# One input projection reordered: all four channel tiles per chunk of tokens, k-tile by k-tile

## The chip, the core and the metric

The kernel runs on one core of a Trainium2 chip. The metric is the device time of one execution in microseconds (us), the median of several runs. The engines of the core work side by side, each with its own queue of instructions: TensorE (PE, with its weight loads shown apart as PEld), VectorE (DVE), ScalarE (ACT), GpSimd (POOL) and SyncE (SP), which here issues most of the transfers. [...]

## The reference

One step of a decoder layer for 1024 prompt tokens and 8 x 8 sample tokens, 1088 rows of 1024 channels. The change touches only the first of the products below, the 512 channels `a`.

```python
u = rms_norm(x, ln1)
a, q, k, v, g_a, g_b = split(u @ w_in)          # w_in: 1024 x 4864; a is 512 wide
branch_a = pooling of a over trailing windows 2/4/8/16, per-group linear map, scale
branch_b = dilated window attention of q, k, v in three groups of heads
h = x + (sigmoid(g_a) * (branch_a @ w_pa) + sigmoid(g_b) * (branch_b @ w_pb)) @ w_o
y = h + relu(rms_norm(h, ln2) @ w_up)**2 @ w_down
```

## The kernel before

Activations are held with channels on the partitions: eight k-tiles of 128 channels by 1088 tokens. For precision, each fp32 operand of a large product is split in two parts, hi (ScalarE, a copy to fp32r) and lo (VectorE, the remainder), and each product is three matmuls: hi x hi, hi x lo, lo x hi. `PASSES` lists them as (weight part, activation part).

The tokens go in three chunks (`CHUNKS`): 384, 384 and 320. The projection to `a` has four output tiles of 128 channels. Two weight panels hold them, 256 channels each: panel a0 gives tiles 0 and 1, panel a1 tiles 2 and 3. A panel is split into one of three `places` in SBUF; its raw fp32 pieces of 128 x 512 (two k-tiles) pass through three `raw` buffers in turn (`fetch`, line 127), so a fourth fetch waits until the first piece has been split (lines 116 and 117). The places are reused in turn by the q, k and v panels of the next stage, whose first matmul on PE is at line 632.

The order of work in the first stage:

- Twelve warm-up matmuls (line 360). Meanwhile x of chunk 0 is loaded, a pair of k-tiles at a time (`load_x`, 384 KB; the first pair as two loads), and panel a0 between.
- Panel a0 over chunks 0, 1, 2: `pool_input(0, wt, c)`, 48 matmuls per chunk (line 334), pair of k-tiles by pair, all passes of a pair before the next. `split_x` (lines 312 and 313) makes the hi and lo parts of a chunk's x. `pool_evac` copies the two tiles out of PSUM (lines 346 and 351).
- Panel a1 over chunks 0, 1, 2 in the same way.
- Between these, `square_x` squares a chunk's x in place on ACT (line 304) and adds the eight k-tiles up on POOL (line 306); `x_sums` then has PE sum over partitions (`rt`, line 369), and VectorE and POOL turn the sums into norms (lines 373 to 375).

PSUM: the accumulators of this stage are four banks in turn. A chunk of one panel uses two of them, so the next chunk finds the other two free.

The order on PE is the order of the program. On the other engines, and on SP, a scheduler at build time sets the order from a simulated timeline; each engine then keeps that order strictly. `behind_pe(instruction, mm)` holds an instruction until a given matmul is done (without `mm`, the last one issued so far). x of chunks 1 and 2 is loaded as early as its place in the SP queue allows.

Of the kernel before, what the change touches and what calls it, by code (L numbers as in the profile page):

```python
# [7 lines left out]
F32 = mybir.dt.float32  # L8
F32R = mybir.dt.float32r
AF = mybir.ActivationFunctionType  # L10
ALU = mybir.AluOpType
# [4 lines left out]
P = 128  # L16
D = 1024
SEQ = 1024
NB, NT = 8, 8
TOK = SEQ + NB * NT  # L20
KD = D // P
CH = 384
# [5 lines left out]
HD = 64  # L28
# [9 lines left out]
def decoder_step(ctx, tc, i, o):  # L38
    nc = tc.nc
    v_, s_, g_, t_ = nc.vector, nc.scalar, nc.gpsimd, nc.tensor  # L40
    dma = nc.sync.dma_start
# [49 lines left out]
    def part4(c):  # L91

        return slice(CHUNKS[c][0] // 4, (CHUNKS[c][0] + CHUNKS[c][1]) // 4)
# [12 lines left out]
    def from4(t, sub="p r l -> p l r"):  # L106
        return t.rearrange("p (r l) -> p r l", r=4).rearrange(sub)
# [4 lines left out]
    place = [0]  # L112
    throttle = []

    def split(dst_hi, dst_lo, src):
        ins = s_.activation(dst_hi, src, AF.Copy)  # L116
        v_.tensor_tensor(dst_lo, src, dst_hi.bitcast(F32), op=ALU.subtract)  # L117
        return ins

    def fetch(src, name, a, tied=False):  # L120
        raw = rr(wp, [P, 512], F32, name=f"raw_{name}_{a}", tag="raw", bufs=3)
        if callable(src):
            ins = dma(raw.rearrange("p (k n) -> p k n", k=4), src(a))
            if tied:
                behind_pe(ins)
        else:
            dma(raw, src[:, a:a + 512])
        return raw
# [121 lines left out]
    def acc_tile(name, tag="acc", bufs=4):  # L250
        return rr(acc_p, [P, 512], F32, name, tag, bufs)
# [17 lines left out]
    def win(name):  # L269
        return rr(xp, [P, LS], F32, name, "win", 2)  # L270
# [17 lines left out]
    def load_x(c, j):  # L288
        c0, n = CHUNKS[c]
        x = rr(xq, [P, 2, CH], F32, name=f"xs{c}_{j}", tag="xs", bufs=12)  # L290
        if c + j == 0:

            dma(x[:, 0, :n], i["xT"][:, 0, c0:c0 + n])
            dma(cols, i["cols"])
        else:
            dma(x[:, :, :n], i["xT"][:, 2 * j:2 * j + 2, c0:c0 + n])
        xs[c, "t", j] = x[:, :, :n]
        for k in range(2):
            xs[c, 2 * j + k] = x[:, k, :n]

    def square_x(c):
        t = [xs[c, "t", j] for j in range(4)]
        for j in (3, 0, 1, 2):
            behind_pe(s_.activation(t[j], t[j], AF.Square))
        for j in range(3):
            g_.tensor_tensor(t[3], t[3], t[j], op=ALU.add)

    def split_x(c, k):
        c0, n = CHUNKS[c]
        hi, lo = (act4[s][k][:, :, part4(c)] for s in range(2))  # L310
        x = xs[c, k].rearrange("p (l r) -> p r l", r=4)
        s_.activation(hi, x, AF.Copy, scale=ln1[:, k:k + 1])  # L312
        v_.scalar_tensor_tensor(lo, x, ln1[:, k:k + 1], hi.bitcast(F32), op0=ALU.mult, op1=ALU.subtract)

    def first(j):
        if j:
            load_x(0, j)
        else:
            dma(xs[0, 1], i["xT"][:, 1, :CH])
        split_x(0, 2 * j)  # L320
        split_x(0, 2 * j + 1)

    L = 15 + SEQ
    LS = L + NB * 23
    exts = {}

    def pool_input(ja, wt, c, middle=None):
        c0, n = CHUNKS[c]
        pts = [acc_tile(f"a{2 * ja + m}_{c}") for m in range(2)]
        for k in range(0, KD, 2):  # L330
            for p, (a, b) in enumerate(PASSES):
                for m in range(2):
                    for kk in (k, k + 1):
                        last_mm[0] = t_.matmul(  # L334
                            pts[m][:, :n], wt[:, a, kk, m * P:(m + 1) * P], act4[b][kk][:, :, part4(c)],
                            start=(p == 0 and kk == 0), stop=(p == 2 and kk == KD - 1))
            if middle and k == 4:
                middle()
        return pts

    def pool_evac(ja, c, pts):
        c0, n = CHUNKS[c]
        for m in range(2):
            ext = exts[2 * ja + m]
            npr = min(n, SEQ - c0)
            s_.copy(ext[:, 15 + c0:15 + c0 + npr].rearrange("p (l r) -> p l r", r=4),
                    from4(pts[m][:, :n])[:, :npr // 4])
            if npr < n:
                new = from4(pts[m][:, :n])[:, npr // 4:].rearrange("p (t q) r -> p q r t", q=2)
                for q in range(2):  # L350
                    s_.copy(ext[:, L:].rearrange("p (b t) -> p b t", b=NB)[:, 4 * q:4 * q + 4, 15:], new[:, q])
# [7 lines left out]
    for _ in range(12):  # L359
        t_.matmul(wu, ones, ones, start=True, stop=True)  # L360
    load_x(0, 0)
    wt = by_k(panel(i["w_in"][0], "a0", first))
    def x_sums(c):
        n = CHUNKS[c][1]
        rt = [rr(ps, [P, 1], F32, name=f"rt{c}_{b}", tag="rt", bufs=3) for b in range(3)]
        for b in range(3):
            w = min(P, n - b * P)
            for k in range(2):
                t_.matmul(rt[b][:w], xs[c, 6 + k][:, b * P:b * P + w], ones[:, :1], start=(k == 0), stop=(k == 1))
        for b in range(3):  # L370
            w = min(P, n - b * P)
            col = slice(3 * c + b, 3 * c + b + 1)
            v_.tensor_scalar(xms[:w, col], rt[b][:w], 1.0 / D, EPS, op0=ALU.mult, op1=ALU.add)
            g_.tensor_tensor(rtok[0][:w, col], xms[:w, col], mhalf[:w, :1], op=ALU.pow)
            v_.tensor_scalar(xeps[0][:w, col], xms[:w, col], EPS, None, op0=ALU.mult)
# [33 lines left out]
            v_.tensor_scalar(xeps[g][:, :8], xg, EPS, None, op0=ALU.mult)  # L409

    v_.memset(rtok[0], 0.0)
    for c in range(3):
        if c < 2:
            for j in range(4):
                load_x(c + 1, j)
        if c == 0:
            open_ext(0)
            open_ext(1)
        pool_evac(0, c, pool_input(0, wt, c))
        if c < 2:  # L420
            for k in range(KD):
                split_x(c + 1, k)
        if c:
            square_x(c - 1)
    square_x(2)
    w1 = by_k(panel(i["w_in"][1], "a1"))
    dma(cst, i["consts"])
    v_.tensor_scalar(wqs, wqc, HD ** -0.5, None, op0=ALU.mult)
    dma(states, i["stateT"].rearrange("g p b t -> p g (b t)"))
    kn = win("kn")[:, :P]  # L430
    for g in range(3):
        dma(kn[2 * g:2 * g + 2], i["qk_norm"][g, 1].rearrange("(j d) -> j d", j=2))
    open_ext(2)
    open_ext(3)
    for c in range(3):
        pool_evac(1, c, pool_input(1, w1, c, (lambda: x_sums(2)) if c == 2 else None))
        if c == 0:
            x_sums(0)
            sample_rows()
        if c == 1:  # L440
            x_sums(1)

            wk = rr(ps, [P, 512], F32, name="wk", tag="wu", bufs=1)[:, :6]
            t_.transpose(wk, kn[:6], ident[:6, :6])
            v_.tensor_tensor(wqk, wqs, wk, op=ALU.mult)
    moving = by_residue()
    next(moving)
    px.close()
# [722 lines left out]
    for g in (2, 1, 0):  # L1171
# [42 lines left out]
        for blks in ((8, 0), (1,), (2,), (3,), (4,), (5,)) + (((6, 7),) if g else ((6,), (7,))):  # L1214
# [12 lines left out]
            for js in (((0, 1), (2,)) if blks[0] in (1, 2, 3, 4, 5) else ((0,), (1,), (2,))):  # L1227
                for b in (blks[::-1] if g < 2 and js == (2,) and 8 in blks else blks):
# [1039 lines left out]
```

## Time and profile before

| | |
|---|---|
| median of 3 runs | 1400.61 us (1399.87 to 1401.57) |
| profiled execution | 1399.09 us, of which the span of the profile is 1397.3 us |
| TensorE busy | 1390.2 us |
| VectorE busy | 954.0 us |
| ScalarE busy | 756.1 us |
| GpSimd busy | 258.3 us |
| first projection matmul | 6.09 us from the span's start |
| first matmul of the next stage (line 632) | 61.03 us |

The profile is of one execution. "Busy" adds up the times in which an engine had an instruction under way; TensorE's matmuls are pipelined and overlap in the list, so the spacing of their starts says what one costs. In a timeline row stand the start, the duration of the (merged) instructions, the engine, the source line, the operation, the tensors written and read, the shapes and the count; in square brackets stands how long the engine was idle before it and who released it. L334 is line 334 of the kernel. A queue that ends in q (SPq) is the issue of transfers, not their landing.

### The profile page before, as it was taken

Reading aid. Unit: us, or ns where it says so; the run is one execution under the profiler, and the core shown is the slowest. Engines: PE = TensorE matmul, PEld = TensorE weight load, DVE = VectorE, ACT = ScalarE, POOL = GpSimd, SP = SyncE. Lnnn points to the kernel's source line nnn. Section 1 sums busy time; section 2 is a strip of 40 time slices with the busy share of each in tenths; the row PEclk is TensorE's granted clock in tenths of the full one; section 3 lists DMA queues with packets and bytes.
Section 4 is the critical chain, followed back from the end, with each engine's and each line's share of the span. In section 5 each row is a group of like instructions: output and inputs, shape, how many; then the busy total and the mean of one; then the engine's idle time right before and its main releaser. Section 6 shows DMA issues by size and latency. Waiting matters only on the chain.

```text
span 1397.3 us, 29307 instructions
## 1 busy us (share of the span) xinstructions
PE 1390.2 (99%) x11101; PEld 1341.6 (96%) x11101; DVE 954.0 (68%) x1707; ACT 756.1 (54%) x1787; POOL 258.3 (18%) x362
## 2 busy tenths in 40 slices
PE   9999999999999999999999999999999999999998
PEld 8988987888999999999999999999999999999998
DVE  7788744776876776975559677765665686664565
ACT  8557875787764224554337454554554544444443
POOL 0854356676500000000010000000000000000100
PEclk9999999999999999999999999999999999999999
DMA  6456886755587777956369668765768987777674
GB/s 216 133 166 211 245 246 195 231 139 137 149 248 232 244 220 257 318 194 211 130 199 296 222 217 290 245 204 204 250 202 287 319 274 257 238 239 230 211 256 170
DMA packets 180445, 311.96 MB, mean 223 GB/s; under 512 B 26696, under 2 KB 82318, under 8 KB 178255
## 3 DMA queue, kind: packets, MB, share of 16 engines
q1 hardware_dynamic: 174670, 258.04, 57.8%
q0 software_dynamic: 5632, 52.04, 11.6%
q8 instruction: 87, 1.43, 0.4%
q14 instruction: 56, 0.45, 0.1%
HBM read 239.94 MB, written 122.12 MB: 259 GB/s over the span
## 4 chain that ended last, share of the span: by engine, by line
PE 98%; ACT 0%; DMA 0%; POOL 0%; SPq 0%; issue 0%; DVE 0%; DVEq 0%
PE pz L1330 24%; PE pd L2113 24%; PE pg L1330 12%; PE ph L205 7%; PE pqk L205 6%; PE pab L1330 5%; PE pv L205 5%; PE a L334 3%; PE pk L205 2%; PE pq L205 2%; PE sg0b L702 1%; PE pog0b L735 1%; PE pl L513 1%; PE tpg0b L721 1%; PE sg1b L702 0%; PE tpg1b L721 0%
## 5 line engine op out<-in xcount | busy, mean ns | idle before, releaser
L2113 PE MATMUL pd<-places 128*128 128x272 f32 x2688 | 331.7, 287 | 0.0
L2113 PEld LDWEIGHTS pd<-places 128*128 128x128 f32 x2688 | 331.6, 188 | 0.0
L116 ACT ACTIVATE places<-raw_d 128x544 fp32r<-128x544 f32 (+1 forms) x176 | 110.6, 646 | 159.1 <-DMA raw_d<-z_d 54.8
L2166 POOL DMA_DIRECT2D out_kv_sample_dram<-in_cache_kv_dram x96 | 46.9, 489 | 791.1 <-ACT places L116 582.2
L117 DVE TENSOR_TENSOR places<-raw_d,places 128x544 fp32r<-128x544 f32 (+1 forms) x176 | 122.4, 710 | 90.8 <-ACT places L116 89.0
L1330 PE MATMUL pz<-act,places 128*128 128x280 f32 (+1 forms) x1080 | 139.4, 287 | 0.0
L1330 PEld LDWEIGHTS pz<-act,places 128*128 128x128 f32 x1080 | 135.9, 188 | 0.0
L205 PE MATMUL ph<-act,places 128*128 128x280 f32 (+1 forms) x768 | 96.6, 287 | 0.0
L205 PEld LDWEIGHTS ph<-act,places 128*128 128x128 f32 x768 | 96.0, 188 | 0.1
L1330 PE MATMUL pg<-act,places 128*128 128x264 f32 (+1 forms) x576 | 75.6, 288 | 0.0
L1330 PEld LDWEIGHTS pg<-act,places 128*128 128x128 f32 x576 | 72.6, 188 | 0.6 <-issue 0.3
L1330 PE MATMUL pz<-places,apart 128*128 128x264 f32 (+1 forms) x528 | 67.9, 287 | 0.0
L1330 PEld LDWEIGHTS pz<-places,apart 128*128 128x128 f32 x528 | 66.6, 188 | 0.0
L205 PE MATMUL pqk<-places,act 128*128 128x512 f32 x240 | 60.6, 402 | 0.0
L1330 PE MATMUL pz<-act,apart 128*128 128x264 f32 (+1 forms) x456 | 59.1, 287 | 0.0
L1330 PEld LDWEIGHTS pz<-act,apart 128*128 128x128 f32 x456 | 57.5, 188 | 0.1
L661 POOL TENSOR_TENSOR mr<-ms,mhalf 128x4 f32<-128x4 f32 (+2 forms) x39 | 54.7, 1403 | 2.9 <-POOL ms L660 0.2
L205 PEld LDWEIGHTS pqk<-places,act 128*128 128x128 f32 x240 | 44.8, 192 | 9.6
L886 POOL TENSOR_TENSOR pck<-pck,qs 128x256 f32<-128x256 f32 x64 | 48.6, 791 | 21.1 <-DVE sta L711 12.4
L334 PE MATMUL a<-act,places 128*128 128x384 f32 (+1 forms) x288 | 50.5, 333 | 1.7 <-ACT act L312 1.1
L334 PEld LDWEIGHTS a<-act,places 128*128 128x128 f32 x288 | 47.6, 188 | 3.8 <-ACT act L312 1.9
L1330 PE MATMUL pab<-ab,places 128*128 128x264 f32 (+1 forms) x384 | 50.4, 286 | 0.0
(438 smaller groups left out, 2805.8 us busy)
## 6 DMA issues: line engine op xcount, KB each, us to landing
out_kv_sample_dram<-in_cache_kv_dram POOLq DMA_DIRECT2D x72, 480.0 KB, 5.0
raw_d<-z_d SPq DMA_DIRECT2D x112, 272.0 KB, 4.2
z_d<-t SPq DMA_DIRECT2D x80, 272.0 KB, 3.7
raw_d<-in_w_down_dram SPq DMA_DIRECT2D x80, 256.0 KB, 4.1
raw_u<-in_w_up_dram SPq DMA_DIRECT2D x64, 256.0 KB, 4.3
raw_qkv<-in_w_in_dram SPq DMA_DIRECT2D x36, 256.0 KB, 4.3
own_d<-in_cache_kv_dram POOLq DMA_DIRECT2D x32, 256.0 KB, 3.8
pck<-own_d SPq DMA_DIRECT2D x16, 512.0 KB, 4.8
```

The lines of the kernel that those rows point to most:

```text
L116: ins = s_.activation(dst_hi, src, AF.Copy)
L117: v_.tensor_tensor(dst_lo, src, dst_hi.bitcast(F32), op=ALU.subtract)
L205: last_mm[0] = t_.matmul(out, lhs(a, k), rhs(b, k), start=(j == 0), stop=(j == len(terms) - 1))
L334: last_mm[0] = t_.matmul(pts[m][:, :n], wt[:, a, kk, m * P:(m + 1) * P], act4[b][kk][:, :, part4(c)], start=(p == 0 and kk == 0), stop=(p ...
L513: t_.matmul(pl[:, :npr], lin[:, g, :], dp_[:, c0:c0 + npr], start=True, stop=True)
L661: last_norm[0] = g_.tensor_tensor(r[:n, :H], ms[:n, :H], mhalf[:n, :H], op=ALU.pow)
L702: t_.matmul(sc[e][:, hp, j * P:(j + 1) * P], qT[rows, hp, :], kT[rows, 2 + hp, :], start=True, stop=True)
L721: t_.transpose(tp[:, hp * nk + j, :], sms[e][:, hp, j * P:(j + 1) * P], ident)
L886: ins = g_.tensor_tensor(out, *others, op=ALU.mult)
L1330: last_mm[0] = t_.matmul(out[c], lhs(*term), rhs(*term, c), start=(first and n == 0), stop=(n == len(terms) - 1), skip_group_check=not first)
L2113: last_mm[0] = t_.matmul(chain[t][c], A[:, a, t * P:(t + 1) * P], Z[:, b, c], start=(fresh and f == 0 and n == 0), stop=(f == NG - 1 and n ...
L2166: ins = g_.dma_start(d, a)
```

## The change

The projection now runs once per chunk with all four tiles, instead of once per panel and chunk. In chunks 0 and 1 the first six k-tiles go pair by pair over both panels and all four accumulators (24 matmuls on a pair), and the last two k-tiles then tile by tile, so that each tile is finished and copied out by itself. Chunk 2 goes tile by tile over all k-tiles. In chunk 0, panel a0, the odd k-tiles take the lo part of the weights ahead of the lo part of x (`BY_WEIGHT`).

Both panels' pieces are fetched in turn with x of chunk 0, whose k-tiles are now loaded singly (192 KB). x of chunk 1 is loaded behind the end of panel a1's matmuls on k-tiles 2 and 3 of chunk 0 (`in_chunk[0, 3]`), x of chunk 2 behind a1's on k-tiles 4 and 5 (`in_chunk[0, 5]`); the hi splits of chunk 1 wait for a0's matmuls on k-tiles 4 and 5 (`in_chunk[0, 4]`). The constants, states and norms are loaded behind the end of chunk 0. The squares and row sums move with the new order: `x_sums` runs after tile 0, after tile 1, and two thirds into tile 3 of chunk 2.

```diff
-            dma(x[:, :, :n], i["xT"][:, 2 * j:2 * j + 2, c0:c0 + n])
+            behind_pe(dma(x[:, :, :n], i["xT"][:, 2 * j:2 * j + 2, c0:c0 + n]), mm)
...
-        s_.activation(hi, x, AF.Copy, scale=ln1[:, k:k + 1])
+        ins = s_.activation(hi, x, AF.Copy, scale=ln1[:, k:k + 1])
+        if c == 1:
+            behind_pe(ins, in_chunk[0, 4])
...
+    def first_panels():
+        wts = []
+        for _ in range(2):
+            wts.append(places[:, place[0] % 3])
+            place[0] += 1
+        for j in range(4):
+            if j:
+                t = rr(xq, [P, 2, CH], F32, name=f"xs0_{j}", tag="xs", bufs=12)
+                xs[0, "t", j] = t
+                for k in range(2):
+                    xs[0, 2 * j + k] = t[:, k]
+                dma(t[:, 0], i["xT"][:, 2 * j, :CH])
+            raw = [fetch(i["w_in"][0], "a0", 512 * j)]
+            dma(xs[0, 2 * j + 1], i["xT"][:, 2 * j + 1, :CH])
+            raw.append(fetch(i["w_in"][1], "a1", 512 * j))
+            for ja in range(2):
+                split_x(0, 2 * j + ja)
+                ins = split(*(wts[ja][:, s, 512 * j:512 * j + 512] for s in range(2)), raw[ja])
+        throttle.append(ins)
+        return [by_k(w) for w in wts]
...
+    BY_WEIGHT = ((0, 0), (1, 0), (0, 1))
...
+        begun = 6 if c < 2 else 0
+        for k in range(0, begun, 2):
+            for ja in range(2):
+                for kk in (k, k + 1):
+                    for p, (a, b) in enumerate(BY_WEIGHT if c == 0 and ja == 0 and kk else PASSES):
+                        for m in range(2):
+                            mm(2 * ja + m, a, b, kk, kk == 0 and p == 0, False)
+                in_chunk[c, k + ja] = last_mm[0]
+        for t in range(4):
+            for p, (a, b) in enumerate(PASSES):
+                for k in range(begun, KD):
+                    mm(t, a, b, k, p + k == 0, p == 2 and k == KD - 1)
+                if p == 1 and (t, 1) in then:
+                    then[t, 1]()
+            pool_evac(t, c, pts[t])
+            if t in then:
+                then[t]()
...
+    THEN = ({}, {0: lambda: split_chunk(2), 1: lambda: square_x(1), 3: lambda: square_x(2)},
+            {0: lambda: (x_sums(0), sample_rows()), 1: lambda: (x_sums(1), key_norms()), (3, 1): lambda: x_sums(2)})
     for c in range(3):
+        pool_input(c, THEN[c])
         if c == 0:
+            for cc in range(1, 3):
+                for j in range(4):
+                    load_x(cc, j, in_chunk[0, 3] if cc == 1 else in_chunk[0, 5])
+            split_chunk(1)
+            square_x(0)
+            behind_pe(dma(cst, i["consts"]))
```

More of the change, by code (lines that the diff above doesn't have):

```diff
@@ L286, in decoder_step, with load_x @@
     xs = {}
-    def load_x(c, j):
+    def load_x(c, j, mm=None):
         c0, n = CHUNKS[c]
@@ L325, in decoder_step, with pool_input @@
     exts = {}
-    def pool_input(ja, wt, c, middle=None):
+    BY_WEIGHT = ((0, 0), (1, 0), (0, 1))
+    in_chunk = {}
+    def pool_input(c, then={}):
         c0, n = CHUNKS[c]
-        pts = [acc_tile(f"a{2 * ja + m}_{c}") for m in range(2)]
-        for k in range(0, KD, 2):
-            for p, (a, b) in enumerate(PASSES):
[L332 to L339, printed above, removed]
@@ L341, in pool_evac @@
-    def pool_evac(ja, c, pts):
-        c0, n = CHUNKS[c]
[L343 to L351, printed above, removed]
+        pts = {}
@@ new lines, in mm @@
+        def mm(t, a, b, k, start, stop):
+            ja, m = divmod(t, 2)
+            if t not in pts:
+                pts[t] = acc_tile(f"a{t}_{c}")
+            last_mm[0] = t_.matmul(pts[t][:, :n], wt[ja][:, a, k, m * P:(m + 1) * P], act4[b][k][:, :, part4(c)],
+                                   start=start, stop=stop)
+        begun = 6 if c < 2 else 0
[6 more added lines that the diff above has]
+                in_chunk[c, k + ja] = last_mm[0]
@@ new lines, in pool_input, with pool_evac @@
+        for t in range(4):
+            for p, (a, b) in enumerate(PASSES):
+                for k in range(begun, KD):
[5 more added lines that the diff above has]
+                then[t]()
+    def pool_evac(t, c, pt):
+        c0, n = CHUNKS[c]
+        ext = exts[t]
+        npr = min(n, SEQ - c0)
+        s_.copy(ext[:, 15 + c0:15 + c0 + npr].rearrange("p (l r) -> p l r", r=4), from4(pt[:, :n])[:, :npr // 4])
+        if npr < n:
+            new = from4(pt[:, :n])[:, npr // 4:].rearrange("p (t q) r -> p q r t", q=2)
+            for q in range(2):
+                s_.copy(ext[:, L:].rearrange("p (b t) -> p b t", b=NB)[:, 4 * q:4 * q + 4, 15:], new[:, q])
@@ L361, in decoder_step @@
     load_x(0, 0)
-    wt = by_k(panel(i["w_in"][0], "a0", first))
+    wt = first_panels()
     def x_sums(c):
```

52 lines of the change are left out of this document (14 added, 38 removed).

## The prediction

> **What bounds the kernel now.** I read the page's totals first, then its chain of work that ended last, then the timeline of the first 61 us engine by engine, because the diff touches nothing behind that point.
>
> ```profile
> span 1397.3 us, 29307 instructions
> PE 1390.2 (99%) x11101; PEld 1341.6 (96%) x11101; DVE 954.0 (68%) x1707; ACT 756.1 (54%) x1787; POOL 258.3 (18%) x362
> PE 98%; ACT 0%; DMA 0%; POOL 0%; SPq 0%; issue 0%; DVE 0%; DVEq 0%
> ```
>
> TensorE sets the time nearly everywhere. The change alters no number of matmuls, so it can only win time in which TensorE stands still between its first projection matmul and the first matmul of the next stage (line 632), or lose by making it stand still more. So I price the real matmuls and compare them with the clock. In the timeline of PE (start, duration, engine, line):
>
> ```profile
> 6.09 0.44 PE L334 MATMUL a<-act,places 128*128 128x384 f32 x1 [0.59 <-ACT places L116]
> 6.98 2.46 PE L334 MATMUL a<-act,places 128*128 128x384 f32 x11 [0.45 <-ACT act L312]
> 9.68 0.44 PE L334 MATMUL a<-act,places 128*128 128x384 f32 x1 [0.24 <-ACT act L312]
> 10.55 30.90 PE L334 MATMUL a<-act,places 128*128 128x384 f32 x179 [0.42 <-ACT act L312]
> 41.29 1.39 PE L369 MATMUL rt<-ones,xs 128*128 128x1 f32 x12
> 42.54 8.73 PE L334 MATMUL a<-act,places 128*128 128x384 f32 x48
> 51.11 1.39 PE L369 MATMUL rt<-ones,xs 128*128 128x1 f32 x12
> 52.58 5.55 PE L334 MATMUL a<-act,places 128*128 128x320 f32 x36
> 57.97 1.27 PE L369 MATMUL rt<-ones,xs 128*128 128x1 f32 x12
> 59.17 2.02 PE L334 MATMUL a<-act,places 128*128 128x320 f32 x12
> 61.03 0.28 PE L632 MATMUL pq<-places,smp_t 128*128 128x256 f32 x1
> ```
>
> Durations overlap, so I go by starts. 48 matmuls of 384 columns take 51.11 - 42.54 = 8.57 us, 0.1785 each; 36 of 320 columns take 57.97 - 52.58 = 5.39, 0.150 each. The projection has 192 of the first and 96 of the second kind: 34.3 + 14.4 = 48.7 us. The row sums (rt) with the small transpose cost 1.25 + 1.47 + 1.20 = 3.9. Work: 52.6 us. Clock: 61.03 - 6.09 = 54.9. So TensorE loses 2.3 us here, and 2.1 of them by 10.55, where 13 matmuls (2.3 us of work) have taken 4.46. **That 2.3 us is the most this change can win.** It lies where each k pair of chunk 0 waits for its split, since before only 12 matmuls (2.1 us) stand on a pair.
>
> **Part 1: chunk 0 with all four tiles.** A k pair now carries 24 matmuls, 4.3 us, but also needs a second panel's piece. These are the splits (ACT hi, DVE lo) and the arrivals:
>
> ```profile
> 5.41 0.63 ACT L116 ACTIVATE places<-raw_a 128x512 fp32r<-128x512 f32 x1 [1.02 <-DMA raw_a<-in_w_in_dram]
> 5.95 0.98 ACT L312 ACTIVATE act<-xs,cols 128x384 fp32r<-128x384 f32 x1
> 7.24 0.63 ACT L116 ACTIVATE places<-raw_a 128x512 fp32r<-128x512 f32 x1 [0.31 <-DMA raw_a<-in_w_in_dram]
> 8.65 1.85 ACT L312 ACTIVATE act<-xs,cols 128x384 fp32r<-128x384 f32 x2 [0.77 <-DMA xs<-in_xT_dram]
> 6.07 0.69 DVE L117 TENSOR_TENSOR places<-raw_a,places 128x512 fp32r<-128x512 f32 x1 [0.74 <-ACT places L116]
> 6.96 0.92 DVE L313 SCALAR_TENSOR_TENSOR act<-xs,cols,act 128x384 fp32r<-128x384 f32 x1 [0.20 <-ACT act L312]
> ```
>
> The first matmul still needs x0 and the first weight piece, whose loads keep their places: 6.09. The order by weight lets the first four matmuls go on x0 alone; only the twelfth needs x1's lo part, ready at 6.96 + 0.92 = 7.88, so twelve are done at about 8.24, with no loss. The second panel's first piece takes the fetch that landed at 7.24. From there ACT needs 0.98 + 0.63 = 1.6 us per k, 12.9 for eight, and DVE 0.92 + 0.69 = 1.6; PE needs 12 x 0.1785 = 2.14 per k. PE is the slower, and chunk 0 would end at 8.24 + 84 x 0.1785 = 23.2. That is the whole 2.3 us, if the transfers keep up.
>
> They are 8 x 192 KB of x and 8 x 256 KB of weights, 3.67 MB. Only three raw buffers turn over; the fourth fetch waits, and x loads queue on SP behind it:
>
> ```profile
> 6.79 0.34 SPq L127 DMA_DIRECT2D raw_a<-in_w_in_dram  x1
> raw_a<-in_w_in_dram SPq DMA_DIRECT2D x8, 256.0 KB, 5.3
> DMA to landing us min/median/max: 2.8/4.3/6.8
> 0.00:5.00 5.00, 3.94 (x21) 3.94 (x22) 1.09 (x9) 2.47 (x3) 0.20 (x4) 1.00 0.48 122
> 5.00:10.00 5.00, 3.72 (x18) 2.53 (x16) 2.98 (x5) 3.50 (x5) 0.00 (x0) 1.00 1.01 342
> ```
>
> (The last two rows are windows; their last column is GB/s.) A buffer's turn is landing + 0.63 + 0.69 us. At 2.8 the fourth fetch, issued at 6.8, is split by 10.9, and PE wants it at 12.5; at the 5.3 that pieces took under the full load of before, it lands at 12.1, and PE waits 0.2 to 1 us on this turn and the next. At 6.8 it would lose about 3. The queue is emptier in the new order, so I take the lower end, a loss of 0.2.
>
> At 342 GB/s the 3.67 MB need 10.7 us, well inside the 17 of chunk 0. [...]
>
> **Part 2: chunk 1 behind chunk 0.** The loads wait on SP for chunk 0's 48th matmul, 8.24 + 36 x 0.1785 = 14.7. Behind them on SP stand chunk 2's loads, the constants, states, norms and then the next stage's weights; none of those is wanted before 40 us. The splits wait on ACT for the 60th matmul, 16.8. With a landing of 2.8, x arrives from 17.5; at 0.98 + 0.92 a pair's splits are done by about 20.4, and PE wants them at 23.2: a cover of 2.8 us, lost only if landing takes 5.6 or more.
>
> The four accumulators are another matter. Before, a chunk used two banks of four and the next had the other two; now all four are full when chunk 1 begins, and its first two matmuls need tiles 0 and 1 copied out. Those copies share ACT with the splits:
>
> ```profile
> 14.97 5.39 ACT L312 ACTIVATE act<-xs,cols 128x384 fp32r<-128x384 f32 x6
> 20.26 0.83 ACT L346 COPY ext<-a 128x384 f32<-128x384 f32 x2
> 20.99 7.96 ACT L312 ACTIVATE act<-xs,cols 128x384 fp32r<-128x384 f32 x10
> ```
>
> Here the copies ran at 20.26 behind six splits of the next chunk, though 48 matmuls were done by about 17.2 (10.55 + 35 x 0.1785 = 16.8 and the last one's 0.34). That cost nothing with two spare banks. In the new order tiles 0 and 1 finish at 20.0 and 21.1. With none of the eight splits ahead the cost is nothing; with six ahead, from 17.5 at 0.90 each, the copies end at 23.7, 0.5 us late; with all eight at 25.5, 2.3 late. I take the middle one, nearest to what ACT's order was: 0.5. [...]
>
> **Part 3: the end.** The row sums of x sit after tile 0, after tile 1 and two thirds into tile 3 of chunk 2. Each needs four squares on ACT and three adds on POOL:
>
> ```profile
> 30.63 3.05 ACT L304 ACTIVATE xs<-xs 128x768 f32<-128x768 f32 x4
> 32.30 16.72 POOL L306 TENSOR_TENSOR xs<-xs,xs 128x768 f32<-128x768 f32 x8 [31.85 <-ACT xs L304]
> 56.45 2.03 POOL L374 TENSOR_TENSOR stats<-stats,mhalf 128x1 f32<-128x1 f32 x3 [1.88 <-DVE stats L373]
> 38.80 2.33 DVE L117 TENSOR_TENSOR places<-raw_qkv,places 128x512 fp32r<-128x512 f32 x1
> 52.25 2.32 POOL L306 TENSOR_TENSOR xs<-xs,xs 128x640 f32<-128x640 f32 x1
> 66.80 0.57 PE L632 MATMUL pk<-places,smp_t 128*128 128x256 f32 x1
> ```
>
> Chunk 1's squares are now held to the end of its tile 1: 23.2 + 84 x 0.1785 = 38.2. The first add can go after two squares, 39.8; six adds of 2.09 (16.72 / 8) end at 52.3, and with both sets of powers ahead of the last one (2 x 2.0) at 56.3. PE reaches the last sums at 40.4 (chunk 1's end) + 88 x 0.150 + 2.7 for the first two sums = 56.3. So the cost is nothing, or, with every add at the 2.32 of the row at 52.25, 1.4 us; I take nothing, since in that row the last add ran ahead of the second powers. While POOL adds, a DVE split takes 2.33 instead of 0.69. Chunk 2's eight lo splits, three of them beside adds at 2.33 and five at 0.92, take 12 us from 25.5, when chunk 1's are done; PE wants them at 40.4, a cover of 3. The panels' places come free after tiles 1 and 3 of chunk 2, at 48.9 and 58.7, and take the next stage's second and third panel. The second is wanted 2 us ahead of the row at 66.80, at 64.5; its four splits need 4 x 2.33 = 9 us at the dearest, a cover of 6, without which each us late would cost one.
>
> **The sum.** 2.3 won, 0.2 for supply and 0.5 for banks lost: 1.6 us. The profiled run took 1399.09 (span 1397.3), 1.5 below the median of 1400.61; the gain counts the same on either, so 1397.5 for that run and 1399.0 for the median. What a measurement of this kernel can tell from no change is about 0.2%, 2.8 us (bounds 1397.8 and 1403.4).
>
> **The rivals.**
> - Banks: all chunk 1 splits go ahead of the copies. For it, the row at 20.26; against it, chunk 1's splits are now held to 16.8. It takes back 2.3: 1400.6.
> - Raw buffers: three do not turn over fast enough, landing stays at 5.3 or above. For it, the 5.3; against it, the queue is no longer full of chunks 1 and 2. A loss of 1 to 3 us: 1399.3 to 1401.3. This is also the case in which the change does not do what it says, as chunk 0 is again paced by arrivals.
> - POOL: slow adds with the powers ahead of the last. For it, the 2.32; against it, the order that POOL kept there. It loses 1.4 us: 1400.4.
> - The slower side: transfer rate. The last weights must land by about 19.8, so 3.67 MB need 185 GB/s from the start. At 165 the win is gone, below 147 the kernel is slower by over 2.8 us, and at the 122 of the first 5 us the last piece lands at 30, 10 late, less the 2.3 won: 1408.5. For it, that window; against it, the next at 342, the first having held the start-up.
>
> **How the numbers follow.** Forecast 0.48, banks 0.15, raw buffers 0.12, POOL 0.09, transfer rate 0.08. The 0.08 left is for a reordering of the other engines further on, which this trace cannot show. Faster by over 0.2% is above the 2.3 us ceiling; it takes the spread of the runs (1399.87 to 1401.57) or a lucky reordering: 0.10. Slower: the transfer rate and a little more, 0.10. Same: 0.80. The range 1397.6 to 1402.2 takes in the full win with 0.7 of spread below, and the bank and buffer cases above.
>
> **What would show it.** Right: chunk 0's 96 matmuls run without a wait from about 8.2 to 23.2, line 632 starts near 59.4, and any wait in between names ACT's copies (the new line of the copy) at 23. Wrong: PE waiting for DMA or the weight split between 10 and 22 (buffers, or rate if under 185 GB/s); a wait of 2 us at the first matmul of chunk 1 (banks); rt waiting for POOL near 56 (adds). If line 632 comes 2 us earlier and the time does not move, the win is given back in the attention stage, and I would be wrong in holding that stage to be PE's.

## The result and the profile after

The changed kernel takes 1408.41 us (median of 6 runs, 1408.02 to 1409.42), the kernel before 1400.24 (6 runs, 1398.9 to 1402.92): a ratio of 1.0056, 95% interval 1.0043 to 1.0069. It is 8 us slower, where I had forecast a gain of 1.6. The profiled run of after took 1408.44 us, span 1406.7, against 1399.09 and 1397.3 before. Its page first: totals, the chain that ended last, and the projection's own group.

```profile
span 1406.7 us, 29320 instructions
PE 1393.7 (99%) x11101; PEld 1345.3 (96%) x11101; DVE 949.9 (68%) x1707; ACT 756.5 (54%) x1787; POOL 260.2 (18%) x362
PE 90%; DMA 3%; DVE 2%; POOL 2%; ACT 2%; issue 1%; SPq 1%; DVEq 0%; POOLq 0%; ACTq 0%
...
L354 PE MATMUL a<-act,places 128*128 128x384 f32 (+1 forms) x288 | 51.1, 338 | 5.1 <-ACT ext L379 4.6
```

The number of matmuls is the same; TensorE is busy 3.5 us longer for them, and the projection's matmuls now stand idle 5.1 us, 4.6 of it for ACT's copies out of PSUM (line 379 now, 346 before). The same stretch in the timeline of PE (line 354 was 334, 401 was 369, 658 was 632):

```profile
6.29 17.21 PE L354 MATMUL a<-act,places 128*128 128x384 f32 x96 [0.50 <-ACT places L116]
26.47 0.45 PE L354 MATMUL a<-act,places 128*128 128x384 f32 x1 [2.96 <-ACT ext L379]
28.58 22.10 PE L354 MATMUL a<-act,places 128*128 128x384 f32 x119 [1.67 <-ACT ext L379]
50.52 1.39 PE L401 MATMUL rt<-ones,xs 128*128 128x1 f32 x12
...
63.69 1.38 PE L401 MATMUL rt<-ones,xs 128*128 128x1 f32 x12 [0.71 <-POOL xs L306]
...
66.27 0.40 PE L658 MATMUL pq<-places,smp_t 128*128 128x256 f32 x1
...
70.27 3.13 PE L205 MATMUL pq<-places,act 128*128 128x256 f32 x24
```

The last of these rows was, before:

```profile
63.48 3.13 PE L205 MATMUL pq<-places,act 128*128 128x256 f32 x24
```

Chunk 0 is what the change meant it to be: 96 matmuls from 6.29 to 23.4 without a wait, 2.3 us won. Then TensorE does one matmul in 5 us. The windows (the last three columns are the granted clock, the DMA share and GB/s) show a second loss behind it:

```profile
25.00:30.00 5.00, 1.86 (x6) 1.61 (x7) 4.32 (x6) 5.00 (x8) 0.00 (x0) 0.87 1.05 382
30.00:40.00 10.00, 10.00 (x53) 10.00 (x52) 6.71 (x9) 10.00 (x16) 5.80 (x3) 0.89 0.41 128
...
60.00:70.00 10.00, 9.29 (x61) 9.00 (x59) 4.37 (x14) 3.69 (x11) 7.22 (x9) 0.83 0.52 158
```

In half-microsecond windows the granted clock is 0.50 from 28.7 to 32.1 and from 66.3 to 69.7, two periods of 3.4 us. Before, it was 1.00 throughout this stretch; the first of the windows was

```profile
25.00:30.00 5.00, 5.00 (x35) 5.00 (x34) 5.00 (x8) 5.00 (x9) 0.00 (x0) 1.00 0.00 0
```

The ledger, in us against before:

| where | us | how it is read |
|---|---|---|
| first matmul | +0.2 | 6.29 against 6.09 |
| chunk 0 | -2.3 | no wait for k pairs any more |
| standstill behind chunk 0 | +5.0 | the second matmul of chunk 1 at 28.58 instead of 23.6 |
| first half-clock period | +1.4 | 28.58 to 50.52 is 21.94; 95 x 0.1785 + 24 x 0.150 = 20.56 |
| last row sums wait for POOL | +0.7 | the row at 63.69 |
| line 658 | **+5.2** | 66.27 against 61.03 |
| second half-clock period | +1.6 | line 205 at 70.27 against 63.48, +6.8 |
| behind it | +2.6 | to +9.4 at the end (1406.7 against 1397.3) |

The five rows ahead of line 658 make up the +5.2 within 0.2. Two of the small waits behind the projection are named in the list of TensorE's waits:

```profile
PE sg0b L728 <- ACT pTg0b L750: 0.9, 1, 0.9
...
PE pab L1356 <- DVE ggf L1677: 0.3, 1, 0.3
```

How the standstill comes about is seen on SP's queue and on ACT:

```profile
16.39 0.93 SPq L127 DMA_DIRECT2D raw_qkv<-in_w_in_dram  x2
17.41 2.53 SPq L296 DMA_DIRECT2D xs<-in_xT_dram  x4
...
20.09 0.63 ACT L116 ACTIVATE places<-raw_qkv 128x512 fp32r<-128x512 f32 x1 [1.36 <-DMA raw_qkv<-in_w_in_dram]
21.30 0.63 ACT L116 ACTIVATE places<-raw_qkv 128x512 fp32r<-128x512 f32 x1 [0.58 <-DMA raw_qkv<-in_w_in_dram]
22.47 3.59 ACT L312 ACTIVATE act<-xs,cols 128x384 fp32r<-128x384 f32 x4 [0.53 <-PE a L354]
25.96 0.45 ACT L379 COPY ext<-a 128x384 f32<-128x384 f32 x1
26.32 1.84 ACT L312 ACTIVATE act<-xs,cols 128x384 fp32r<-128x384 f32 x2
28.07 0.46 ACT L379 COPY ext<-a 128x384 f32<-128x384 f32 x1
```

Two fetches of the q panel stand ahead of chunk 1's x on SP, so x is issued at 17.41, not at the 14.7 of my sum. Its first split starts at 22.47, and the copies of tiles 0 and 1, whose sums were done by 21.3 (84 matmuls of chunk 0), run behind four and six splits. (PE's matmul, named as the releaser at 22.47, was the 60th, done since 17.0; so the wait must be for the transfer of x, which the rows of two variants, hold_qkv and sq_early, name at this place.)

### The profile page after: what moved, and what is told of

The parts are those of the page before. It is cut to its first block, busy times and chain, and to the rows that moved or that the text cites. A ratio compares the mean times of both kernels' runs of the same rounds, so it can differ in the third digit from the quotient of the medians.

```text
span 1406.7 us, 29320 instructions
## 1 busy us (share of the span) xinstructions
PE 1393.7 (99%) x11101; PEld 1345.3 (96%) x11101; DVE 949.9 (68%) x1707; ACT 756.5 (54%) x1787; POOL 260.2 (18%) x362
## 4 chain that ended last, share of the span: by engine, by line
PE 90%; DMA 3%; DVE 2%; POOL 2%; ACT 2%; issue 1%; SPq 1%; DVEq 0%; POOLq 0%; ACTq 0%
PE pz L1356 23%; PE pd L2139 23%; PE pg L1356 11%; PE ph L205 7%; PE pqk L205 5%; PE pv L205 4%; PE pab L1356 4%; PE a L354 3%; PE pq L205 1%; PE pk L205 1%; POOL pcv L912 1%; DMA raw_ab<-in_w_ab_dram 1%; DMA pcv<-in_cache_kv_dram 1%; DMA raw_qkv<-in_w_in_dram 1%; PE pl L539 1%
```

## The experiments

My theory: the loss is ACT's order, copies behind splits that themselves came late because of SP's order, with no spare bank; the half clock follows from the standstill. Rivals: the holds themselves cost the time; the later stages, ordered anew at every build, cost it; a fresh order of squares and adds does. All variants below start from after unless said otherwise. "Next stage" is the start of its first matmul in the profile. "Behind it" is how much longer than before the profiled run takes from there to its end (1336.3 us before). The ratio is against before on the same chip; the runs were made on several chips, so ratios compare better than medians.

| run | next stage, us | behind it, us | median, us | ratio, 95% |
|---|---|---|---|---|
| before (profile shown above) | 61.0 | | 1400.24 | |
| after | 66.3 | +4.2 | 1408.41 | 1.0043 to 1.0069 |
| no_holds | 67.4 | +3.3 | 1408.62 | 1.0049 to 1.0074 |
| hold_qkv | 67.5 | +0.3 | 1407.84 | 1.0047 to 1.0074 |
| copy_first | 68.8 | +2.9 | 1409.47 | 1.0048 to 1.0073 |
| hold_copy | 69.2 | +3.1 | 1410.25 | 1.0055 to 1.0081 |
| hold_copy_sq | 70.1 | +0.1 | 1410.33 | 1.0060 to 1.0085 |
| sq_early | 67.6 | +0.5 | 1405.65 | 1.0027 to 1.0054 |
| junk | 65.9 | +1.0 | 1408.38 | 1.0042 to 1.0067 |
| six_banks | 67.4 | +6.0 | 1410.41 | 1.0063 to 1.0089 |
| all_copies | 65.9 | +5.0 | 1407.49 | 1.0034 to 1.0061 |
| all_copies_x | 69.1 | +1.9 | 1408.86 | 1.0043 to 1.0068 |
| all_copies_x_sq | 64.0 | +2.8 | 1403.61 | 1.0013 to 1.0031 |
| best | 61.5 | +4.1 | 1404.32 | 1.0024 to 1.0051 |
| best_mid | 63.0 | +1.0 | 1402.06 | 1.0003 to 1.0022 |
| before_f3 (from before) | 66.3 | +1.2 | 1403.07 | 0.9999 to 1.0029 |
| before_f32 (from before) | 71.3 | +10.7 | 1414.66 | 1.0075 to 1.0104 |

### Are the holds the loss? (no_holds)

```diff
-            behind_pe(dma(x[:, :, :n], i["xT"][:, 2 * j:2 * j + 2, c0:c0 + n]), mm)
+            dma(x[:, :, :n], i["xT"][:, 2 * j:2 * j + 2, c0:c0 + n])
...
-        if c == 1:
-            behind_pe(ins, in_chunk[0, 4])
```

> The changed kernel without any hold on the loads of chunks 1 and 2 and on the splits of chunk 1. In this build chunk 1's x goes out between the weight pieces of chunk 0, and ten to twelve splits stand ahead of pieces of panel a1 and of the copies. Theory: the holds are needed, since chunk 0 then waits again for its own weights (1 to 3 us from 10 to 23 us) and the copies end 2 us late or more; chunk 1's data is early: 1405 to 1409. Rival hold points: the holds make the loss, and without them it goes: 1400 to 1402.

TensorE's waits:

```profile
PE a L352 <- ACT places L116: 4.7, 3, 3.1
...
PE a L352 <- ACT ext L377: 0.5, 1, 0.5
```

Without the holds chunk 1's x comes between the panel pieces, and on ACT six of its splits (17.80 to 23.16) run ahead of the split of such a piece. TensorE waits 4.7 us for these pieces instead of 4.6 for the copies. The holds do what they are for; they are not the loss.

### The q panel on SP (hold_qkv)

The q panel's first fetch waits for chunk 0's last matmul.

```diff
+            ins = dma(raw, src[:, a:a + 512])
+            if name == "qkv2_0":
+                behind_pe(ins, held_by[0])
...
+    held_by = [None]
...
         if c == 0:
+            held_by[0] = last_mm[0]
```

> The changed kernel with the next stage's first panel (q) fetched only behind chunk 0's last matmul, so that chunk 1's x stands ahead of it on SP and its splits ahead of the panel's on ACT. Theory late data: x of chunk 1 goes out at 14.9 us instead of 17.4 and the splits begin near 18 instead of 22.5; in this build six splits stand ahead of tile 0's copy and eight ahead of tile 1's, so the copies end near 23.9 and 26.1, PE stands still 2.7 us instead of 5.0, and if the clock then stays up another 1.4 comes back: 1404.5 to 1406.1. Rival banks alone (the copies' place on ACT decides, not when x comes): a gain of 1 us or less, about 1407.5.

```profile
15.28 6.09 SPq L299 DMA_DIRECT2D xs<-in_xT_dram  x8
...
20.75 5.33 ACT L315 ACTIVATE act<-xs,cols 128x384 fp32r<-128x384 f32 x6 [1.83 <-DMA xs<-in_xT_dram]
25.99 0.46 ACT L382 COPY ext<-a 128x384 f32<-128x384 f32 x1
```

x now goes out at 15.28, 2.1 us earlier, and its splits start 1.7 earlier, still 5.5 us behind the issue. The copy comes at the same 26 us, because six splits instead of four now run ahead of it. That half of my theory falls: earlier data alone buy nothing while ACT's order puts splits first.

### Copies ahead of splits (copy_first, hold_copy, hold_copy_sq)

Chunk 1's splits from k-tile 2 on wait for tile 1's end in chunk 0; hold_copy adds the held q panel, hold_copy_sq also chunk 1's squares right behind chunk 0's.

```diff
-            behind_pe(ins, in_chunk[0, 4])
+            behind_pe(ins, in_chunk[0, 4] if k < 2 else in_chunk[0, "t1"])
...
+            in_chunk[c, f"t{t}"] = last_mm[0]
```

> The changed kernel with chunk 1's splits from k-tile 2 on held behind tile 1 of chunk 0, so that on ACT the copies of tiles 0 and 1 stand behind two splits instead of four and six; x still comes late. Theory banks: PE gets banks 0 and 1 near 25.2 instead of 26.4 and 28.5 and starts chunk 1 there: 3.3 us back, 1405.1, or 1403.6 if the clock stays up. Rival late data alone: chunk 1 cannot start much earlier whatever the copies do, 1407.5 to 1408.4.

> Both of the two edits before: x of chunk 1 on time and the copies behind two splits. If the two causes together make the standstill, PE runs from chunk 0 into chunk 1 without a gap at about 23.4, the clock does not fall at 28.7, and 5.0 + 1.4 us come back: 1402.0; what stays is the wait for POOL ahead of the last row sums with its clock (2.4) and what is lost behind the projection (2.6). Rival hold points (the holds on PE are too late by themselves): 2 us or more of standstill stay, 1404 or above.

> As the kernel before it, and chunk 1's squares are no longer held to its tile 1 but go right behind chunk 0's. POOL's adds for chunk 1 then run ahead of time, the last row sums do not wait (0.8 us) and the clock does not fall behind them (1.5): 1399.7. If what was lost behind the projection (2.6 us) was the scheduler's new order and is not there in this build: down to 1397.5. Rival: the squares were not what the last sums waited for, and nothing changes against the kernel before it (1402).

All three missed. In hold_copy, ACT and then PE:

```profile
23.12 0.83 ACT L383 COPY ext<-a 128x384 f32<-128x384 f32 x2
23.85 6.88 ACT L315 ACTIVATE act<-xs,cols 128x384 fp32r<-128x384 f32 x8
30.64 0.45 ACT L383 COPY ext<-a 128x384 f32<-128x384 f32 x1
...
31.14 0.69 PE L357 MATMUL a<-act,places 128*128 128x384 f32 x1 [4.91 <-ACT ext L383]
33.03 19.92 PE L357 MATMUL a<-act,places 128*128 128x384 f32 x107 [1.20 <-ACT ext L383]
```

The copies of tiles 0 and 1 are out by 24 and chunk 1 begins without a gap, but after 12 matmuls it needs tiles 2 and 3, and their copies stand behind eight splits: waits of 4.91 and 1.20 us in place of 2.96 and 1.67. The wait moved by one pair of tiles, which shows that all four copies count, not the first two.

### All four copies first (all_copies, all_copies_x)

```diff
-        if c == 1:
-            behind_pe(ins, in_chunk[0, 4])
+        if c:
+            behind_pe(ins, in_chunk[1, 0] if c == 2 else in_chunk[0, 4] if k < 2 else in_chunk[0, "end"])
...
+            in_chunk[c, "end"] = last_mm[0]
```

> The changed kernel with chunk 1's splits from k-tile 2 on held behind the end of chunk 0 and chunk 2's behind chunk 1's first pair, so that on ACT all four copies of chunk 0 stand behind two splits of chunk 1 only; x still comes late. In the kernel that held the splits behind tile 1 alone, PE got tiles 0 and 1 but then waited for the copies of tiles 2 and 3 behind six more splits. Theory banks and late data: the copies end between 24.8 and 27, PE starts chunk 1 near 25.2 and loses 1.8 to 2.5 instead of 5.0, with the clock up if the phase allows: 1404 to 1406. Rival: something else than the copies holds chunk 1, 1408.

> The same, and the next stage's first panel is fetched behind chunk 0, so that chunk 1's x goes out at 15.3 (its first piece was split at 20.75 in the run with that edit). Two splits end at 22.6, the four copies at 24.3. Theory: PE goes from chunk 0 into chunk 1 at 23.4 with 0.5 us of waiting at most, the clock stays at 1.00 there, 4.5 to 6 us come back in the projection: its end near 60 to 61, the time 1402 to 1403.5 with what is lost at the last sums and behind the projection. Rival: the second-panel tiles wait again, or chunk 1's later pairs for splits, and less than 3 us come back.

all_copies: one wait of 1.88 us behind chunk 0, first row sums at 48.2 instead of 50.5. all_copies_x, with the q panel held too, has no standstill behind chunk 0 at all (PE):

```profile
5.95 38.76 PE L357 MATMUL a<-act,places 128*128 128x384 f32 x216
44.55 1.39 PE L405 MATMUL rt<-ones,xs 128*128 128x1 f32 x12
46.95 3.79 PE L357 MATMUL a<-act,places 128*128 128x320 f32 x24 [1.01 <-ACT ext L383]
55.54 2.72 PE L405 MATMUL rt<-ones,xs 128*128 128x1 f32 x12 [4.80 <-POOL xs L309]
```

The first row sums are 6.0 us earlier than in after, of the 6.4 that standstill and half clock had cost, by order alone. That shows their cause. But 4.8 us are lost again at the second row sums: POOL gets chunk 1's squares only at 48.46 and has chunk 2's first add ahead of chunk 1's last. The order was the same in after, where PE came there later and did not wait. The time as a whole is therefore no better (1.0055 against after's 1.0056).

### Squares early (sq_early, all_copies_x_sq)

```diff
-    THEN = ({}, {0: lambda: split_chunk(2), 1: lambda: square_x(1), 3: lambda: square_x(2)},
+    THEN = ({}, {0: lambda: split_chunk(2), 3: lambda: square_x(2)},
...
             square_x(0)
+            square_x(1)
```

> The changed kernel with chunk 1's squares right behind chunk 0's instead of behind tile 1 of chunk 1. Theory: the last row sums waited for POOL's adds, which began too late; without that, the 0.8 us wait goes and with it the half clock from 66.3 to 69.7 (1.5): 1406.0. Rival: the powers on POOL, not the late squares, hold the last adds back, and the wait stays: 1408.4.

> The same with chunk 1's squares right behind chunk 0's. The wait of the last row sums goes as well; the projection ends near 59 to 60, 1 to 2 us ahead of the kernel before. Theory that the losses of the change all lie in the projection: 1398 to 1399.5, at or under the kernel before. Rival: what the scheduler does to the stages behind it (0.3 to 6 us in the profiles so far) remains and the time stays at 1401 or above although the projection is short.

In sq_early the row sums no longer wait for POOL, and no half clock follows them. It takes 1405.65 us, near the 1406.0 expected; against before it is 1.0041, where after is 1.0056, some 2 us less, with intervals that overlap. That the forecast was met is partly luck. In the profile the half clock behind chunk 0 lasts two periods instead of one (28.7 to 35.6), the next stage starts 1.3 us later than in after, and the gain lies behind that line: 0.5 us lost there instead of 4.2, of which the half clock explains 1.6. With the copies first as well it is 1403.61. In that profile one wait is left in the projection, between chunks 1 and 2, for copies that stand behind three splits of the q panel:

```profile
44.09 5.31 PE L357 MATMUL a<-act,places 128*128 128x320 f32 x24 [2.66 <-ACT ext L383]
```

### Spare banks (six_banks)

Tiles 0 and 1 of chunk 1 get two banks of their own, and the three row sums of a chunk share one.

```diff
-    spare, held = [0], [0]
+    spare, held = [0], [1]
...
-                pts[t] = acc_tile(f"a{t}_{c}")
+                pts[t] = rr(ps, [P, 512], F32, f"a{t}_{c}", "spare", 2) if c == 1 and t < 2 else acc_tile(f"a{t}_{c}")
...
-        rt = [rr(ps, [P, 1], F32, name=f"rt{c}_{b}", tag="rt", bufs=3) for b in range(3)]
+        rts = rr(ps, [P, 512], F32, name=f"rt{c}", tag="rt", bufs=1)
+        rt = [rts[:, 8 * b:8 * b + 1] for b in range(3)]
```

> The changed kernel with two spare accumulator banks for tiles 0 and 1 of chunk 1 (the row sums share one bank for that). Theory banks: chunk 1's first twelve matmuls no longer wait for ACT's copies, only for the splits, and run from 23.5; tiles 2 and 3 take the banks of chunk 0's tiles 0 and 1 and wait for the copy that ends at 28.5. So 2.1 us come back, 3.5 to 3.8 if the clock stays up: 1404.6 to 1406.3. Rival late data alone: 0.3 us or less, 1408.1.

```profile
24.48 0.62 PE L354 MATMUL a<-act,places 128*128 128x384 f32 x2 [0.97 <-ACT act L312]
...
29.59 18.72 PE L354 MATMUL a<-act,places 128*128 128x384 f32 x107 [1.66 <-ACT ext L379]
48.15 1.39 PE L402 MATMUL rt<-ones,xs 128*128 128x1 f32 x12
...
54.35 1.91 PE L402 MATMUL rt<-ones,xs 128*128 128x1 f32 x12 [1.19 <-DVE stats L408]
```

At the start of chunk 1 the wait is now 0.97 us and for a split, not for a copy, and the first row sums come 2.4 us earlier, 1.4 of it for a half-clock period that does not come: the missing banks are part of the cause. The wait at the row sums, which now share a bank, is then 1.19, and from the k panel's first matmul to the end 6.0 us are lost against before (2.6 in after), 3.0 of them in two waits for ACT (`pg`, line 1357). So the total does not tell what spare banks are worth.

### The half clock (junk)

Adds 20 matmuls into a bank that nobody reads, between chunks 0 and 1.

```diff
-    wu = rr(ps, [P, 512], F32, name="wu", tag="wu", bufs=1)[:, :P]
+    wuf = rr(ps, [P, 512], F32, name="wu", tag="wu", bufs=1)
+    wu = wuf[:, :P]
...
+        for _ in range(20 if c == 0 else 0):
+            t_.matmul(wuf[:, :384], wt[0][:, 0, 0, :P], act4[0][0][:, :, part4(0)], start=True, stop=True)
```

> The changed kernel with 20 matmuls of 128x384 between chunks 0 and 1 that write a bank nobody reads (they add work and change no result). They fill 3.6 us of the 5 us in which PE stands still. Theory clock: the half clock from 28.7 to 32.1 is there because PE stood still, so the clock stays at 1.00 and 1.4 to 1.7 us come back: 1406.8. Rival: the clock has another cause, and the time stays at 1408.4 or grows by up to 0.5 us since the first matmul of chunk 1 comes after the added ones.

```profile
25.00:30.00 5.00, 3.86 (x22) 3.44 (x20) 4.31 (x6) 5.00 (x9) 0.00 (x0) 1.00 1.04 378
30.00:40.00 10.00, 9.03 (x50) 8.63 (x49) 6.71 (x9) 10.00 (x16) 5.79 (x3) 1.00 0.36 115
```

The copies keep their order and the standstill is filled up to two waits of 1.14 and 0.97 us: the clock stays at 1.00, here and at the end of the projection. The other runs leave no trace, but each has its mean granted clock: 1.000 in four of the five, against 0.996 to 0.998 in all six of after (one period of 3.41 us at half takes 0.0012 off). So the half clock behind chunk 0 as an effect of the standstill is shown.

The time does not come back with it. The profiled run is 3.5 us faster than after's, but only 0.4 of that lies ahead of the next stage, since the added matmuls take time themselves, and the median is the same (1408.38; 1404.97 to 1408.76). Of the runs at 1.000, three took 1406.47, 1408.67 and 1408.76: what they lose against the profiled one is not the half clock, and it stays open what it is. One thing more: the row sums wait for POOL here too (0.74 us, 0.71 in after), and no half clock follows.

### What a late projection costs by itself (before_f3, before_f32)

The kernel before, with 3 or 32 matmuls more that nobody reads between the first panel's second and third chunk.

```diff
-    wu = rr(ps, [P, 512], F32, name="wu", tag="wu", bufs=1)[:, :P]
+    wuf = rr(ps, [P, 512], F32, name="wu", tag="wu", bufs=1)
+    wu = wuf[:, :P]
...
         pool_evac(0, c, pool_input(0, wt, c))
+        for _ in range(3 if c == 1 else 0):
+            t_.matmul(wuf[:, :384], wt[:, 0, 0, :P], act4[0][0][:, :, part4(0)], start=True, stop=True)
```

> The kernel before with 3 matmuls of 128x384 more (0.161 us each by its own profile's pace, 0.5 us in all), whose sums nobody reads, between the first panel's second and third chunk. If the later stages keep their order when the projection shifts a little: +0.5 us, 1400.1 us or so beside 1399.6. If every edit lays the later stages anew with a loss or gain of some us: anything from 1397 to 1404 us, with the first matmul behind the projection only 0.5 us later.

> The same with 32 such matmuls, 5.2 us: the shift of after's projection without after's order of it. If a late projection passes through to the end as it is: 1404.8 us beside 1399.6, and every later stage 5.2 us later. If a shift of 5 us costs more behind the projection by itself, because the later stages are laid anew: as late as after, 1407 to 1409 us. If later transfers and other slack take up some of it: under 1403 us.

before_f3, PE and a window:

```profile
52.87 2.22 PE L370 MATMUL rt<-ones,xs 128*128 128x1 f32 x12 [0.73 <-DVE stats L374]
...
50.00:60.00 10.00, 9.19 (x43) 8.69 (x43) 7.41 (x34) 3.17 (x6) 7.36 (x7) 0.71 0.40 123
```

before_f32, PE:

```profile
25.93 5.78 PE L422 MATMUL wu<-act,places 128*128 128x384 f32 x32
31.55 15.63 PE L334 MATMUL a<-act,places 128*128 128x320 f32 x96
...
59.48 1.80 PE L370 MATMUL rt<-ones,xs 128*128 128x1 f32 x12 [2.33 <-DVE stats L374]
```

This I had not expected. Half a microsecond of filler makes the row sums wait 0.73 us for VectorE, two half-clock periods follow (54.2 to 61.0), and the next stage starts 5.3 us late in the profile. That run is the slowest of nine (1405.55), and not typical: five others have a mean clock of 1.000, so no full period of half clock, and take 1399.67 to 1404.40. The ratio is 1.0014, about 2 us, with an interval that just reaches no change.

32 fillers take 5.6 us (31.55 - 25.93) and cost 10.3 at the next stage (2.3 for the row sums, 1.5 for a half-clock period at 61.6 to 65.1) and 0.90% of the time, 12.6 us. So a delay of the projection can cost more than its own length, with none of the change in the kernel.

It need not. By the table's column "behind it", hold_copy_sq starts the next stage 9.1 us late and loses 0.1 more to the end, hold_qkv 6.5 late and 0.3; best is 0.5 late and loses 4.1, six_banks 6.3 late and 6.0. The loss behind the line does not follow the delay. It differs from build to build, and after's (4.2, of which 1.6 are the second half-clock period) lies inside that spread. So the rest of it needs no cause of its own in the change, but no run shows what it is made of.

### The cures together (best, best_mid)

all_copies_x_sq with the q panel's fetch behind chunk 1's end (best), or behind the first six k-tiles of chunk 1 (best_mid, shown).

```diff
+            if name == "qkv2_0":
+                behind_pe(ins, held_by[0])
...
                 in_chunk[c, k + ja] = last_mm[0]
+                if c == 1:
+                    held_by[0] = last_mm[0]
```

> The version that puts the cures together: chunk 1's splits from k-tile 2 on and chunk 2's splits held so that ScalarE copies out all four tiles of the chunk that just ended before it splits on, the q panel's three pieces fetched behind chunk 1's end, chunk 1's squares right behind chunk 0's. If the loss sits in ScalarE's copies and in what stands ahead of the loads on SP: no gap at 23 us, under 1 us between chunks 1 and 2, the first matmuls behind the projection (pq) at 59 to 61 us against 61.0 before and 66.3 after, and a time of 1397.5 to 1400.5 us if nothing is lost behind the projection. If the order of the later stages, laid anew at every build, decides: pq as early as that, and still 1401 us or more. If the half clock follows short rests of TensorE: one or two 3.4 us periods at 0.5 remain near the row sums, 1.5 us each.

> best with the q panel's fetch behind the first part of chunk 1's matmuls (36 us) instead of behind all of them (41 us). If the q panel's late pieces make best's loss between the projection and the k panel (2.3 us there, by VectorE's splits of them ahead of the last row sums' scaling): k panel's first matmul at 67 to 68 us against 69.1 in best, and 1400 to 1402.5 us. If the loss behind the projection comes of the order of the later stages: 1403 us or more again.

best reaches the next stage at 61.5 us, within half a microsecond of before, and is still 4.7 us slower: the q panel's pieces now come so late that VectorE's splits of them stand ahead of the last scaling of the row sums, and k's first matmul comes 2.3 us late. best_mid, where k starts 5.8 us behind q as before (7.6 in best), is the fastest version, 1402.06 us. But its k panel starts at 68.8, only 0.3 earlier than in best and not at the 67 to 68 expected; most of what it wins on best lies further behind. Its PE, and a window:

```profile
42.03 3.79 PE L357 MATMUL a<-act,places 128*128 128x320 f32 x24 [1.13 <-ACT ext L385]
...
51.16 1.80 PE L407 MATMUL rt<-ones,xs 128*128 128x1 f32 x12 [0.49 <-DVE stats L411]
...
50.00:60.00 10.00, 9.44 (x55) 9.06 (x54) 9.54 (x35) 3.01 (x10) 7.81 (x9) 0.83 0.33 108
```

Waits of 1.13 and 0.49 and one half-clock period (54.3 to 57.7, 1.5 us) are what is left in the projection, more than the 2.3 won in chunk 0. Its ratio of 1.0013 is that of before_f3 (1.0014) with its 0.5 us of filler. No version that beats the kernel before was found.

## Why the prediction was wrong

- **The ceiling and chunk 0: right.** The 2.3 us were there and were won, with no wait for transfers (0.2 forecast). The buffer and transfer-rate rivals did not come; my only slower rival was the wrong one. (Two counts are off, without effect: the first six matmuls, not four, go on x0 alone, and the eleventh, not the twelfth, is the first on x1's lo part.)
- **"Behind them on SP stand ... then the next stage's weights": failed.** They stood ahead. I read the order of the program, while SP's order is the build's; x went out 2.7 us late (17.41 against 14.7). hold_qkv shows that curing this alone does not help.
- **"With a landing of 2.8 ... a cover of 2.8 us": failed.** From issue to first split it took 5.1 us here and 5.5 in hold_qkv, at the edge that I had named as the end of the cover (5.6). The 2.8 is the least of a row that is not of x: 2.8/4.3/6.8 is the view of line 127, the weight pieces of 256 KB. The larger loads of x had rows of their own before (the list of transfers, and the view of line 296), above that edge:

```profile
xs<-in_xT_dram SPq DMA_DIRECT2D x7, 384.0 KB, 6.2
DMA to landing us min/median/max: 6.2/6.7/7.2
```

- **"I take the middle one ... 0.5": the step that decided it.** The mechanism was right and named (copies on ACT behind splits, no spare bank), the size was not: 5.0 us, outside my bounds of 0 to 2.3. What was mis-sized is the start of the splits, 17.5 in my sum and 22.47 in the run: 2.7 of the difference is SP's order, 2.3 the landing. With the measured start my own sum of six splits and two copies gives 22.47 + 6 x 0.90 + 0.83 = 28.7, and the second copy ended at 28.53. An earlier start alone is no cure: in hold_qkv eight splits stand ahead of that copy instead of six. I also left tiles 2 and 3 out, which cost nothing in after and 4.9 us in hold_copy.
- **The clock: a term that was missing.** I took 0.1785 us per matmul throughout. The two half-clock periods cost 1.4 and 1.6 us in the profiled run, and junk shows by filling the gap that the first follows from the standstill. The second does not follow from the wait ahead of it alone (0.71 us), since junk has that wait (0.74) and keeps the clock at 1.00.
- **"So the cost is nothing" at the last row sums:** 0.7 us, and the second half-clock period behind it makes 2.3, beyond my dear end of 1.4. It came as the POOL rival said, with the powers (60.03 to 62.11) ahead of the last add. sq_early takes the wait away.
- **"A reordering of the other engines further on", 0.08:** 2.6 us of the profiled run. The builds from after lose 0.1 to 6.0 us behind the projection, whatever its delay. Which reordering takes them in after is not settled: 0.9 at sg0b and 0.3 at pab are named waits, the rest is spread.

## What to carry to other kernels

When a reordering fills every accumulator, price each copy-out at its place in the order of the engine that does it, behind all that this order puts first, and read that order from a build, not from the program. Take the time of a transfer from the row of that transfer, not from another that is smaller. Price a standstill of TensorE at its length, and allow for a half-clock period behind it, which cost 1.4 and 1.6 us in after. And run the kernel before with a neutral filler once: here 0.5 us of filler moved the time by about 2 us, at the edge of the noise, and the stages behind the projection differ by up to 6 us between builds, so a gain of 2 us in one stage could hardly be read off the total.

## What the runs showed of the hardware

- In after the granted clock was 0.50 for two periods of 3.41 us. The one from 28.73 begins 0.15 us behind the end of the standstill (28.58), the one from 66.28 2.6 us behind the end of the row sums' wait of 0.71 us (63.69). In best_mid a shorter wait went ahead of one: the period from 54.3 to 57.7 follows a wait of 0.49 us, twelve one-column row sums, a transpose and 1.3 us of full matmuls.
- Waits of nearly one length went with a half clock or without: 0.71 us ahead of the last row sums in after, with the period from 66.28 behind it; 0.74 in junk and 0.7 in no_holds at the same place, with the clock at 1.00 for more than 3 us from the wait's end. No run here was made to find what decides it.
- The last stage of before_f32 ran slower at a granted clock of 1.00. The groups by line, before_f32 and then before:

```profile
L2116 PE MATMUL pd<-places 128*128 128x272 f32 x2688 | 340.6, 289 | 0.0
```

```profile
L2113 PE MATMUL pd<-places 128*128 128x272 f32 x2688 | 331.7, 287 | 0.0
```

  397 matmuls instead of 407 or 408 in every 50 us from 1100 to 1350, 8.9 us over the stage, in the profiled run, which at 1420.11 was the slowest of five (the fastest 1411.07). From its first matmul's start to its last one's the stage took 340.4 us there and 331.4 to 332.1 in twelve other profiles; its cause is open.
- Builds scatter differently: all_copies_x_sq runs from 1400.35 to 1406.44 (11 runs), sq_early from 1404.93 to 1406.07 (5). Why is open, too; in junk runs of one mean clock (1.000) are 3.8 us apart, so the half clock is not all of it.
